# The sample outputs of three heads turned by VectorE blocks and GpSimd DMAs instead of TensorE transposes

## The chip, the cores and the metric

The kernel runs on one core of a Trainium2 chip. The metric is the device time of one execution in microseconds (us). Engines are named as the profile does: PE is TensorE (PEld its weight loads), DVE is VectorE, ACT is ScalarE, POOL is GpSimd, SP is SyncE, which here only issues DMAs.

## The reference, cut to what matters

One inference step of a two-layer decoder on a group of 256 prompt tokens and a group of 64 sample tokens (8 sequences of 8). Layer 0 mixes tokens by gated linear attention with four heads (key width 256, value width 512), layer 1 by a gMLP; each is followed by an MLP. The change lies in layer 0, in what follows the attention of the sample tokens:

```python
o = (jnp.einsum('bhtk,bhkv->bhtv', q_dec, s)
     + jnp.einsum('bhts,bhsv->bhtv', scores, vi))
...
o = o * lax.rsqrt(jnp.mean(jnp.square(o), axis=-1, keepdims=True) + HEAD_NORM_EPS) * norm_g
o = o.reshape(bsz, t, GLA_VAL_DIM).astype(x.dtype) * jax.nn.silu(r)
return o @ w_out, s_fin.astype(s0.dtype)
```

So for each head and token the 512 output values are squared and averaged, and the values are scaled by the inverse root of that mean before they go into the output projection.

## The kernel before, in words

Activations lie transposed in SBUF: features on the 128 partitions, the 320 tokens (256 prompt, 64 sample) along the free axis. Every projection is a run of **weight units**: `unit` loads 512 KB of float32 weights by a DMA of SyncE (`raw`, three buffers), ScalarE rounds them to `wh` (L144), VectorE makes the remainder `wl` (L145), each in a ring of four buffers, and TensorE does 24 matmuls with a unit (`mm3`, L161 to L163: low weights by high data, high by low, high by high). `group` runs over the units of one or two blocks of 256 columns and evicts the sums at the end.

The attention of a head is cut into **steps** (`Head.steps`), which are laid between the weight units. `Side` holds the list and is called after each unit; it takes `ceil(steps left / calls left)` steps from the front. The steps of head h run beside the projections `project_r` of head h and `project_v` of head h+1, 16 calls in all; those of the last head beside its `project_r` and the first two units of the output projection, 10 calls. The order of steps of a head: scores of sample and prompt tokens, then 16 sample steps (8 sequences by 2 key halves) with four prompt steps among them, then `sample_o`, `weigh`, `finish`.

A sample step (`sample_step`) adds into the PSUM tile `hd.po` the query times the carried state (L631, twice), makes the new state (L634 on TensorE, L635 on VectorE) and, for the second key half, stores it from the GpSimd queue (L638). `po` then holds tokens on the partitions and 512 values along the free axis: 64 rows of one partial sum and 64 rows of a second one, for the rounded part and the remainder. `sample_o` brings this into the layout of the rest: ScalarE copies `po` to `os_` (L643); TensorE transposes four 128x128 blocks (L646); ScalarE copies one partial sum to `o_all` (L649); VectorE adds the other (L650); ScalarE squares (L652); VectorE sums the four value blocks into `s1` (L653); a matmul with ones sums over the partitions (L656); `rsqrt` follows. `weigh` (L537) and `finish` (L543) scale `o_all`.

`gather` (L421) is an existing helper: after VectorE has transposed each 32x32 block in place of a full transpose, 16 DMAs (four calls with q = 0 to 3, four DMAs each) carry the blocks to the right partitions. It serves `va` (values, 32 KB a DMA) and `kz`, `ktp` (keys, 16 KB a DMA), on the GpSimd queue, in the last head partly on SyncE's.

Tiles of one tag share its buffers, one buffer in pool `gp`. So `os_` and the squares of the prompt lie in the buffer `sq`, and `kip` (prompt keys of a head, written by L427) has one buffer. The framework adds the waits. It also sets the **order in each engine's queue**: it is asked to plan with simulated times (`schedule_with_timeline_sim=True`, L1126), takes what it believes ready, and prefers what comes first in the program. On the chip each queue runs in that fixed order.

Of the kernel before, what the change touches and what calls it, by code (L numbers as in the profile page):

```python
# [8 lines left out]
F32 = mybir.dt.float32  # L9
# [6 lines left out]
P = 128  # L16
# [6 lines left out]
H = 4  # L23
DK, DV = 256, 512
# [53 lines left out]
def step_kernel(ctx: ExitStack, tc: tile.TileContext, A):  # L78
    nc = tc.nc
    uid = [0]  # L80

    def nm(s):
        uid[0] += 1
        return f"{s}_{uid[0]}"
# [22 lines left out]
    def gltile(n=512):  # L107
        return gl.tile([P, n], F32, tag="gl", name=nm("gl"), padded_shape=[P, 512])
# [4 lines left out]
    ident = cp.tile([P, P], F32, tag="ident", name="ident")  # L113
# [68 lines left out]
    def rsqrt(out, src, scale, eps, eps_t, pool):  # L182

        w = pool.tile([P, T], F32, tag="nw", name=nm("nw"), bufs=1)
        y = pool.tile([P, T], F32, tag="ny", name=nm("ny"), bufs=1)
        nc.scalar.activation(y[:], src, AF.Abs_reciprocal_sqrt, bias=eps_t[:], scale=scale)
        nc.vector.tensor_scalar(w[:], src, -0.5 * scale, -0.5 * eps, op0=ALU.mult, op1=ALU.add)
        nc.vector.tensor_mul(w[:], w[:], y[:])
        nc.vector.tensor_mul(w[:], w[:], y[:])
        nc.vector.scalar_tensor_tensor(out, w[:], 1.5, y[:], op0=ALU.add, op1=ALU.mult)  # L190
# [23 lines left out]
    gp = gst.enter_context(tc.tile_pool(name="gp", bufs=1))  # L214
# [120 lines left out]
    class Head:  # L335
# [284 lines left out]
        def sample_step(hd, b, kt):  # L620
# [16 lines left out]
            if kt == 1:  # L637
                nc.gpsimd.dma_start(SO[b, hd.h].rearrange("(k p) v -> p k v", p=P), st[:])  # L638

        def sample_o(hd):  # L640
            h, s1 = hd.h, hd.s1
            os_ = gp.tile([P, DV], F32, tag="sq", name=nm("os"))
            nc.scalar.copy(os_[:], hd.po[:])  # L643
            pt = gltile()
            for vt in range(4):
                nc.tensor.transpose(pt[:, vt * P : (vt + 1) * P], os_[:, vt * P : (vt + 1) * P], ident[:])  # L646
            pv = pt[:].rearrange("p (v c t) -> p v c t", v=4, c=2)
            o_s = o_all[:, 4 * h : 4 * h + 4, TP:T]
            nc.scalar.copy(o_s, pv[:, :, 0, :])  # L649
            nc.vector.tensor_add(o_s, o_s, pv[:, :, 1, :])  # L650
            sq = g2.tile([P, 4, DB * DS], F32, tag="vfm", name=nm("sq"), bufs=1)
            nc.scalar.activation(sq[:], o_s, AF.Square)  # L652
            nc.vector.tensor_reduce(s1[:, TP:T], sq[:].rearrange("p v t -> p t v"), axis=AX.X, op=ALU.add)  # L653

            pr = gltile(T)
            nc.tensor.matmul(pr[:], ones[:], s1[:], start=True, stop=True)  # L656
            hd.rs = gp.tile([P, T], F32, tag="rs", name=nm("rs"))
            rsqrt(hd.rs[:], pr[:], 1.0 / DV, HEAD_EPS, eps_h, gp)

        def steps(hd):  # L660

            yield hd.sample_scores
            yield hd.prompt_scores
            yield hd.sample_first
            sample = [lambda b=b, kt=kt: hd.sample_step(b, kt) for b in range(DB) for kt in range(2)]
            prompt = {0: lambda: hd.prompt_o(0), 2: lambda: hd.prompt_o(1),
                      12: lambda: hd.prompt_state(0), 14: lambda: hd.prompt_state(1)}
            for i, x in enumerate(sample):
                if i in prompt:
                    yield prompt[i]  # L670
                yield (lambda x=x, q=i - 4: (hd.gather_k(q), x())) if 0 <= i - 4 < 4 else x
            yield hd.sample_o
            yield hd.weigh
            yield hd.finish
# [330 lines left out]
    for j in range(KT):  # L1005
        if j % 4 == 0:
            steps.append(lambda j=j: mix4(j))
        steps.append(lambda j=j: mixed(j, *mix(j)))
    side = Side(steps, 6 * NU)
    ph, pl = yh, yl  # L1010

# [45 lines left out]
    for j in range(KT):  # L1057
# [5 lines left out]
        else:  # L1063
            if j not in ps:
                put_d(j)
            t = l2.tile([P, T], F32, tag="t", name=nm("t"), bufs=3)
# [70 lines left out]
```

## Time and profile before

| | |
|---|---|
| median of 3 runs | 2693.67 us (2693.67 to 2694.58) |
| the profiled execution | 2693.64 us |
| its span, first to last instruction | 2691.9 us |
| mean granted TensorE clock | 0.999 |
| TensorE busy | 2683.6 us |
| VectorE / ScalarE / GpSimd busy | 1547.4 / 1164.8 / 187.9 us |
| mean DMA rate | 164 GB/s |

The four heads lie in the first 450 us or so of the span; the `os_` copies of L643 start between 133.9 and 441.3 us. A row of a timeline gives start, length, engine, line, operation, what it writes and reads, how often, and in brackets how long its engine stood idle before it and what ended that. A row of a line's own view gives shortest, median and longest duration in ns. A row of waits names the waiting engine, tile and line, whom it waited for, the total in us, how often and the longest. A row of a stretch gives its bounds and length, then busy time and number of instructions of TensorE, its weight loads, VectorE, ScalarE and GpSimd, then the clock, the DMA share and GB/s. The row of a kind of DMA gives the size of one and the median time from issue to landing.

### The profile page before, as it was taken

The page shows a single profiled execution, that of the slowest core. Times are in us where ns is not written, and L with a number is a line of the kernel's source. Part 1 is how long each engine was busy: PE and PEld are TensorE (multiplying, and loading weights), DVE is VectorE, ACT ScalarE, POOL GpSimd, SP SyncE. Part 2 cuts the span into 40 slices and gives each one's busy share as a digit, 9 for nine tenths or more (in the row PEclk, how much of TensorE's full clock was granted, in tenths as well). Part 3 has the DMA queues.
Part 4 walks back from the last instruction along what each step waited for, and adds up shares of the span by engine and source line. Part 5 has one row for each costly group of instructions (what it writes and reads, how often), then busy time and mean ns, then how long its engine had stood idle before and what let it go on. Part 6 is the DMA issues. An engine that isn't in the chain of part 4 may idle for free.

```text
span 2691.9 us, 44835 instructions
## 1 busy us (share of the span) xinstructions
PE 2683.6 (100%) x18419; PEld 2661.3 (99%) x18419; DVE 1547.4 (57%) x2305; ACT 1164.8 (43%) x1646; POOL 187.9 (7%) x323
## 2 busy tenths in 40 slices
PE   9999999999999999999999999999999999999999
PEld 9999999999999999999999999999999999999998
DVE  7677677885445444444478765686444444444446
ACT  5455455564234334323446554355324333333434
POOL 4353341000000000000001000000000000000000
PEclk9999999999999999999999999999999999999999
DMA  8667667545444444445545544455445444444442
GB/s 252 220 196 249 218 193 258 187 141 163 151 151 154 150 154 152 153 153 151 155 148 158 160 139 139 136 164 151 155 149 155 151 152 154 150 156 149 153 153 79
DMA packets 136381, 440.84 MB, mean 164 GB/s; under 512 B 19824, under 2 KB 25840, under 8 KB 136176
## 3 DMA queue, kind: packets, MB, share of 16 engines
q1 hardware_dynamic: 121440, 408.08, 48.8%
q0 software_dynamic: 14192, 29.25, 3.5%
q8 instruction: 144, 2.36, 0.4%
q10 hardware_dynamic: 544, 0.66, 0.1%
q14 instruction: 61, 0.50, 0.1%
HBM read 409.60 MB, written 22.02 MB: 160 GB/s over the span
## 4 chain that ended last, share of the span: by engine, by line
PE 99%; DMA 0%; ACT 0%; DVE 0%; ACTq 0%; issue 0%; DVEq 0%
PE mm L161 32%; PE mm L163 32%; PE mm L162 31%; PE gl L631 1%; PE gl L634 1%; PE gl L589 1%; PE gl L980 0%; PE gl L573 0%; DMA raw<-gla_w_in 0%; ACT z L1070 0%; PE gl L975 0%; DMA xr<-xT 0%; PE gl L558 0%; PE gl L603 0%; PE gl L574 0%; PE gl L552 0%
## 5 line engine op out<-in xcount | busy, mean ns | idle before, releaser
L145 DVE TENSOR_TENSOR wl<-raw,wh 128x1024 fp32r<-128x1024 f32 (+1 forms) x740 | 901.0, 1219 | 944.4 <-ACT wh L144 942.5
L144 ACT CAST wh<-raw 128x1024 fp32r<-128x1024 f32 (+1 forms) x740 | 771.2, 1044 | 1231.5 <-PE mm L163 1121.3
L163 PE MATMUL mm<-yh,wh 128*128 128x320 f32 x2624 | 805.0, 307 | 0.0
L161 PE MATMUL mm<-yh,wl 128*128 128x320 f32 x2624 | 803.1, 308 | 0.0
L162 PE MATMUL mm<-yl,wh 128*128 128x320 f32 x2624 | 794.2, 303 | 0.0
L161 PE MATMUL mm<-hh,wl 128*128 128x320 f32 x2048 | 630.8, 308 | 0.0
L163 PE MATMUL mm<-hh,wh 128*128 128x320 f32 x2048 | 628.7, 307 | 0.0
L162 PE MATMUL mm<-hl,wh 128*128 128x320 f32 x2048 | 619.6, 303 | 0.0
L162 PEld LDWEIGHTS mm<-yl,wh 128*128 128x128 f32 x2624 | 492.6, 188 | 0.0
L161 PEld LDWEIGHTS mm<-yh,wl 128*128 128x128 f32 x2624 | 491.0, 188 | 0.0
L163 PEld LDWEIGHTS mm<-yh,wh 128*128 128x128 f32 x2624 | 490.8, 187 | 0.0
L162 PEld LDWEIGHTS mm<-hl,wh 128*128 128x128 f32 x2048 | 384.5, 188 | 0.0
L161 PEld LDWEIGHTS mm<-hh,wl 128*128 128x128 f32 x2048 | 384.4, 188 | 0.0
L163 PEld LDWEIGHTS mm<-hh,wh 128*128 128x128 f32 x2048 | 383.0, 187 | 0.0
L161 PE MATMUL mm<-xh,wl 128*128 128x320 f32 x768 | 237.9, 311 | 0.6 <-ACT xh L230 0.4
L163 PE MATMUL mm<-xh,wh 128*128 128x320 f32 x768 | 236.3, 309 | 0.0
L162 PE MATMUL mm<-xl,wh 128*128 128x320 f32 x768 | 235.2, 306 | 0.0
L162 PEld LDWEIGHTS mm<-xl,wh 128*128 128x128 f32 x768 | 144.2, 188 | 4.6 <-issue 1.2
L161 PEld LDWEIGHTS mm<-xh,wl 128*128 128x128 f32 x768 | 144.0, 188 | 4.7 <-issue 0.7
L163 PEld LDWEIGHTS mm<-xh,wh 128*128 128x128 f32 x768 | 143.6, 187 | 2.6 <-issue 0.7
L421 POOL DMA_DIRECT2D va<-blk x128 | 73.9, 585 | 79.9 <-DVE blk L482 52.0
L889 DVE TENSOR_TENSOR hl<-f,hh 128x320 fp32r<-128x320 f32 x128 | 61.9, 487 | 29.4 <-ACT hh L888 29.4
(261 smaller groups left out, 2209.7 us busy)
## 6 DMA issues: line engine op xcount, KB each, us to landing
raw<-mlp_w SPq DMA_DIRECT2D x512, 512.0 KB, 3.5
raw<-gla_w_in SPq DMA_DIRECT2D x94, 512.0 KB, 4.2
raw<-sg_w_in SPq DMA_DIRECT2D x64, 512.0 KB, 3.6
st<-state SPq DMA_DIRECT2D x32, 512.0 KB, 5.4
o_state_s<-st POOLq DMA_DIRECT2D x32, 512.0 KB, 4.1
raw<-gla_w_out SPq DMA_DIRECT2D x32, 512.0 KB, 4.4
raw<-sg_w_out SPq DMA_DIRECT2D x32, 512.0 KB, 3.5
va<-blk POOLq DMA_DIRECT2D x128, 32.0 KB, 4.3
```

What stands on the lines that cost most here:

```text
L144: nc.scalar.copy(hi[:, ks, :], raw[:, ks, :])
L145: nc.vector.tensor_sub(lo[:, ks, :], raw[:, ks, :], hi[:, ks, :].bitcast(F32))
L161: nc.tensor.matmul(ps, wl[:, kk, s], x_h, start=first, stop=False)
L162: nc.tensor.matmul(ps, wh[:, kk, s], x_l, start=False, stop=False)
L163: nc.tensor.matmul(ps, wh[:, kk, s], x_h, start=False, stop=last)
L421: queue.dma_start(out[32 * q : 32 * (q + 1), :, i, :], src[32 * i : 32 * (i + 1), :, q, :])
L589: nc.tensor.matmul(pairs(pu), hd.ktp[:, kt, blk, :], hd.v_prompt(blk), start=(blk == 0), stop=(blk == 1))
L631: nc.tensor.matmul(po[:], qm[:, kt, b * P : (b + 1) * P], part[:], start=False, stop=(b == DB - 1 and kt == 1 and part is sth))
L634: nc.tensor.matmul(pairs(pu), kz[:, i, kt, g, :], hd.v_sample(g), start=True, stop=True)
L889: nc.vector.tensor_sub(hl[:, j, 0:T], f[:], hh[:, j, 0:T].bitcast(F32))
```

## The change

`sample_o` is split. A new step `sample_out` copies `po` to `os_`; for the first three heads VectorE transposes its 32x32 blocks into `ob` (in the buffer of `kip`), and 16 GpSimd DMAs gather them into `ot` (in the buffer `sq`). Three steps that do nothing follow. `sample_o` then adds the two partial sums from `ot` in one VectorE instruction, and goes on as before. The last head keeps TensorE's transposes, made in `sample_out`, and has no empty steps.

```diff
+        def sample_out(hd):
+
+            os_ = gp.tile([P, DV], F32, tag="sq", name=nm("os"))
+            nc.scalar.copy(os_[:], hd.po[:])
+            if hd.h < H - 1:
+                ob = gp.tile([P, DV], F32, tag="kip", name=nm("ob"))
+                nc.vector.transpose(ob[:], os_[:])
+                hd.ot = gp.tile([P, DV], F32, tag="sq", name=nm("ot"))
+                for q in range(4):
+                    hd.gather(hd.ot[:], ob[:], q)
+            else:
+                hd.ot = gltile()
+                for vt in range(4):
+                    nc.tensor.transpose(hd.ot[:, vt * P : (vt + 1) * P], os_[:, vt * P : (vt + 1) * P], ident[:])
+
         def sample_o(hd):
             h, s1 = hd.h, hd.s1
-            os_ = gp.tile([P, DV], F32, tag="sq", name=nm("os"))
-            nc.scalar.copy(os_[:], hd.po[:])
-            pt = gltile()
-            for vt in range(4):
-                nc.tensor.transpose(pt[:, vt * P : (vt + 1) * P], os_[:, vt * P : (vt + 1) * P], ident[:])
-            pv = pt[:].rearrange("p (v c t) -> p v c t", v=4, c=2)
+            pv = hd.ot[:].rearrange("p (v c t) -> p v c t", v=4, c=2)
             o_s = o_all[:, 4 * h : 4 * h + 4, TP:T]
-            nc.scalar.copy(o_s, pv[:, :, 0, :])
-            nc.vector.tensor_add(o_s, o_s, pv[:, :, 1, :])
+            if h < H - 1:
+                nc.vector.tensor_add(o_s, pv[:, :, 0, :], pv[:, :, 1, :])
+            else:
+                nc.scalar.copy(o_s, pv[:, :, 0, :])
+                nc.vector.tensor_add(o_s, o_s, pv[:, :, 1, :])
...
+            yield hd.sample_out
+            if hd.h < H - 1:
+                for _ in range(3):
+                    yield lambda: None
             yield hd.sample_o
             yield hd.weigh
             yield hd.finish
```

## The prediction

> **What bounds the kernel now.** I read the page's first part, then who waited for whom on TensorE.
>
> ```profile
> span 2691.9 us, 44835 instructions
> PE 2683.6 (100%) x18419; PEld 2661.3 (99%) x18419; DVE 1547.4 (57%) x2305; ACT 1164.8 (43%) x1646; POOL 187.9 (7%) x323
> PE 99%; DMA 0%; ACT 0%; DVE 0%; ACTq 0%; issue 0%; DVEq 0%
> PE gl L152 <- DVE ones L116: 1.1, 1, 1.1
> PE mm L161 <- ACT xh L230: 0.4, 1, 0.4
> PE mm L161 <- DVE wl L145: 0.2, 1, 0.2
> ```
>
> TensorE is busy from end to end, the chain that ended last runs 99% through it, and in the whole span it waited for others for 1.7 us, all of it at the start-up lines or once for a weight. So the time is the number of TensorE's instructions times their spacing. An edit can gain what it takes off that queue; it can lose as much as it makes that queue wait, without limit. The work that hides everything else is the stream of weight units.
>
> **What leaves TensorE.** Twelve of the sixteen transposes of L646 go (four for each of three heads). Their rows, then the second head's four with their neighbours on TensorE, and the later sum over partitions (L656):
>
> ```profile
> L646 PEld LDWEIGHTS gl<-ident,os x16: 141/142/143, 137.2 to 444.8; 128*128 128x128 f32 x16
> L646 PE MATMUL gl<-ident,os x16: 272/273/273, 137.3 to 444.9; 128*128 128x128 f32 x16
> 242.59 0.30 PE L162 MATMUL mm<-xl,wh 128*128 128x320 f32 x1
> 242.74 0.31 PE L163 MATMUL mm<-xh,wh 128*128 128x320 f32 x1
> 242.88 0.60 PE L646 MATMUL gl<-ident,os 128*128 128x128 f32 x4
> 243.24 0.39 PE L161 MATMUL mm<-xh,wl 128*128 128x320 f32 x1
> 243.47 0.31 PE L162 MATMUL mm<-xl,wh 128*128 128x320 f32 x1
> 249.25 0.70 PE L656 MATMUL gl<-s,ones 128*128 128x320 f32 x2
> ```
>
> Matmuls start 0.145 us apart (242.59, 242.74), so without the transposes the L161 would start at 242.88 and the L162 at 243.03. It starts at 243.47. Four transposes therefore cost 0.44 us of the queue, not the 4 x 0.273 = 1.09 us that their lengths add up to, since they overlap one another and their neighbours. Three heads: **-1.3 us**. This is the one term with a sign that I am sure of.
>
> The Trainium skill, "TensorE: Matmul & The Clock Gate", Part 4 on PE-mode transpose, gives about 275 ns for a transpose inside a kernel. The record's 273 ns agrees with it as a length; taken as a price, it would make the gain 12 x 0.275 = 3.3 us. The spacing of the starts decides here, and I take 1.3.
>
> **What is added, and the chain it makes.** Per head: one VectorE block transpose of 128x512 (`ob`), 16 GpSimd DMAs of 16 KB, and a VectorE add that now waits for those DMAs. ScalarE's copy of `o_s` goes. The nearest rows: VectorE's transposes of half the width, the gathers of the same size and layout (`kz`, `ktp`), the rows of ScalarE and VectorE around the second head's sums, and the busy times of that stretch.
>
> ```profile
> 234.30 0.45 DVE L473 STREAM_TRANSPOSE blk<-mm 128x256 f32<-128x256 f32 x1
> L421 POOL DMA_DIRECT2D va<-blk x128: 582/582/640, 39.7 to 372.4; - x128
> L421 POOL DMA_DIRECT2D ktp<-blk x48: 548/549/569, 78.5 to 300.4; - x48
> ktp<-blk POOLq DMA_DIRECT2D x48, 16.0 KB, 3.3
> 239.43 0.58 ACT L643 COPY os<-gl 128x512 f32<-128x512 f32 x1
> 242.65 1.05 ACT L144 CAST wh<-raw 128x1024 fp32r<-128x1024 f32 x1 [2.64 <-PE mm L163]
> 243.60 0.36 ACT L649 COPY o_all<-gl 128x256 f32<-128x256 f32 x1
> 243.73 1.23 DVE L145 TENSOR_TENSOR wl<-raw,wh 128x1024 fp32r<-128x1024 f32 x1 [2.67 <-ACT wh L144]
> 244.87 0.41 DVE L650 TENSOR_TENSOR o_all<-o_all,gl 128x256 f32<-128x256 f32 x1
> 245.77 0.62 DVE L653 TENSOR_REDUCE s<-sq 128x64 f32<-128x256 f32 x1 [0.48 <-ACT sq L652]
> 274.35 0.41 DVE L427 TENSOR_TENSOR kip<-mm,ei 128x256 f32<-128x256 f32 x1
> 226.00:262.00 36.00, 36.00 (x235) 34.40 (x235) 27.47 (x49) 21.19 (x32) 15.97 (x27) 1.00 0.74 234
> ```
>
> *Engine time.* VectorE: 2 x 0.45 = 0.9 us per head, 2.7 us in all, beside 27.47 busy of 36. ScalarE: -0.36 us per head. GpSimd: 16 x 0.549 = 8.8 us per head, 26 in all, beside 15.97 of 36. DMA: 0.26 MB per head beside 234 GB/s x 36 us = 8.4 MB, 3% more. None of these engines is the bound, so I put all at nothing; the cover is the stream of weight units on TensorE, and without it they would cost their own lengths.
>
> *Where the steps fall.* A step is called after each weight unit: 24 matmuls, 24 x 0.145 = 3.5 us. For the first three heads 26 steps over 16 calls become 30. By the rule in `Side`, the last sample step sat after the 13th call and now sits after the 12th, with `sample_out` behind it; the empty steps fill the 13th call and half of the 14th; `sample_o` is after the 14th call, as before. So the chain starts 3.5 us earlier and gets two units, 7 us, between `os` and the sums. For the last head 26 steps become 27 over 10 calls: the last sample step moves one call up, and `sample_out` and `sample_o` fall into one call, with the same instructions as before. I price that at nothing, -0.5 to +0.5 us, as TensorE's total there is unchanged.
>
> *The chain in the second head, by the clock of the profile.* `os` ended at 240.0; 3.5 us earlier is 236.5. `ob` 0.9 us with a little for the hand-over: 237.5. Sixteen issues of 0.549 us: 246.3. The last lands 3.3 us later: **249.6**. From the add's start to the reduction's end took 244.87 to 246.39, 1.5 us, so the sums would be ready at **251.1** if the DMAs come first in GpSimd's queue. The sum's matmul stood at 249.25 in TensorE's queue. If the planner left it there, TensorE would wait 1.9 us; with the copy and the transposes gone the planner could even bring it about 1.5 us forward, to 247.8, and the wait would be 3.3 us.
>
> *What stands in front on GpSimd.* The next head's first sixteen `va` gathers wait for the same last sample step, and the last state store stands among them:
>
> ```profile
> 239.43 7.53 POOL L421 DMA_DIRECT2D va<-blk  x13 [7.97 <-PE gl L634]
> 247.49 0.72 POOL L638 DMA_DIRECT2D o_state_s<-st  x1 [0.53 <-issue]
> 248.21 1.75 POOL L421 DMA_DIRECT2D va<-blk  x3
> 257.44 4.60 POOL L421 DMA_DIRECT2D va<-blk  x8 [7.49 <-DVE blk L482]
> ```
>
> From 239.43 to 249.96 is 10.5 us, less 0.5 idle: 10.0. If all of it is queued ahead of the new sixteen, everything above is up to 9.5 us later: landed at about 259, sums at 260.6. If the new ones go first, `va` is 8.8 us later: done at about 256, when the next batch is not before 257.44, so nobody waits. `ob` lies in the slot of `kip`, which is next written at 274.35, beyond both cases.
>
> *Who waits behind the add.* VectorE's add holds up its `wl` splits, and ScalarE's square holds up its `wh` casts. The cast at 242.65 was let go by TensorE's finishing a unit, and fills a buffer four units on: TensorE reads it after three more units, about 242.65 + 3 x 3.5 + 1.0 = 254.1, while `wl` ended at 244.96. So VectorE can stand for some 9 us there before the weights are late (an estimate from these rows). The sum's matmul has no such reserve: TensorE's queue is in order.
>
> *Does the planner know?* It placed each engine's instructions by its own times, and the add and the sum's matmul move back if it expects the DMAs to land late. What it thinks a gather takes shows in the first head, where it slipped `ktp` gathers between state stores:
>
> ```profile
> 87.75 0.74 POOL L638 DMA_DIRECT2D o_state_s<-st  x1 [4.97 <-DVE st L635]
> 88.50 2.73 POOL L421 DMA_DIRECT2D ktp<-blk  x5
> 94.97 0.72 POOL L638 DMA_DIRECT2D o_state_s<-st  x1 [3.75 <-DVE st L635]
> 95.69 1.66 POOL L421 DMA_DIRECT2D ktp<-blk  x3
> 99.39 0.72 POOL L638 DMA_DIRECT2D o_state_s<-st  x1 [2.04 <-DVE st L635]
> ```
>
> Four more `ktp` gathers were still to come at 91, yet it put only five between stores 7.2 us apart and three between stores 4.4 us apart, and on the chip GpSimd stood idle 3.75 and 2.04 us after them. So it reckons about 1.2 us a gather, twice the chip's 0.55. Then it expects the sixteen to take some 19 us, and puts add and sum later than the chip needs them. Against it: thirteen `va` gathers stand ahead of the store at 247.49, whose data were there at about 239.9; at 1.2 us each that fits badly, and at 0.1 us well. The five-and-three pattern gives the price more directly, so I take **0 us** for the wait, and keep 3.3 to 12.8 us per head as the other end (251.1 and 260.6 less 247.8).
>
> A second rule speaks against the change. The gathers of the trace ran beside a VectorE busy 76% of the stretch above, and the slowest of the 128 `va` took 640 ns where the median took 582. The Trainium skill, "SBUF — State Buffer", section "SBUF: two separate sides", says that certain VectorE copies lock GpSimd out while it writes descriptors, with 620 ns growing to 3100 ns. By it, as an estimate, the sixteen could take 16 x 3.1 = 50 us; no issue in these rows does that.
>
> **The sum.** -1.3 (transposes) + 0 (engines, DMAs, last head) + 0 (wait) = -1.3 us. The profiled execution took 2693.64 us (span 2691.9 and 1.7 around it), the median of the runs is 2693.67, the same to 0.03. Forecast **2692.3 us**, 0.05% under. A change of 0.2% is 5.4 us: about what a measurement of this kernel can tell from none.
>
> **The rivals.**
> *A late gather stops TensorE.* The planner keeps the sum's matmul near 248 on this clock, and the chip's DMAs land after 246.3. Three heads at 3.3 to 12.8 us: +10 to +38, less 1.3: **2702 to 2731 us**, likeliest at the low half, about 2710. It decides from the point at which the sum's matmul is planned earlier than 13.6 us after `ob` is written. For it: the thirteen `va`. Against it: the price of 1.2 us.
> *The gain isn't kept.* TensorE's 0.44 us per head come back as short waits on the re-planned queue (a table load, a step in another place): **2693.6**.
> *The transposes are worth their length.* 12 x 0.273 = 3.3 us: **2690.4**. Against it: the spacing of the starts.
> *GpSimd slowed by VectorE.* The longest gap inside a run of gathers in the first head is quoted here, on top of the issue's own 0.58:
>
> ```profile
> 136.07 6.33 POOL L421 DMA_DIRECT2D va<-blk  x11 [1.47 <-issue]
> ```
>
> If every one of the sixteen met that, each would take 2.05 us, 33 us together: landed at 273.8, sums at 275.3, against 249.25 a wait of 26 us per head: **2770 us**. It happened once, so the chance is small. The SBUF page of the Trainium skill, cited above, leads to the same place.
>
> **How the numbers follow.** Forecast 0.70 (own range 2691.0 to 2693.5), gain not kept 0.08, transposes at full length 0.05, late gather 0.13, GpSimd slowed 0.02, and 0.02 for a gain above 5.4 us, for which I see no work to remove. Slower by over 0.2% takes the late gather and the slowed GpSimd: 0.15. Within 0.2% (2688.3 to 2699.1): 0.70 + 0.08 + 0.05 = 0.83. Faster: 0.02. The range takes the first three cases and a late gather that is mostly hidden: 2690.4 to 2700.0.
>
> **What would show it.** Twelve L646 records fewer and four left. In the second head: `os` near 236, `ob` one 128x512 transpose of about 0.9 us, sixteen gathers of 0.55 us, landing 12 us after the first issue; the add and the sum's matmul later than 249.25, at 251 or beyond, with no idle of TensorE before it. Wrong if TensorE waits at the sum's matmul or for a `wl` around 245 to 262 and its like in the other heads, or if GpSimd's issues stretch beyond 0.64 us.

## The result, and the profile after

The changed kernel takes **2737.51 us** (2736.65 to 2738.09, 4 runs) against 2693.73: a ratio of 1.0161, 95% interval 1.0149 to 1.0173. It is 43.8 us slower; the forecast was 2692.3. Its profiled execution took 2737.76 us.

From the page and from TensorE's waits over the whole span (engine and line, whom it waited for; us in total, times, longest):

```profile
span 2736.0 us, 44875 instructions
PE 2687.4 (98%) x18407; PEld 2665.5 (97%) x18407; DVE 1552.7 (57%) x2308; ACT 1166.0 (43%) x1643; POOL 214.2 (8%) x371
PE mm L161 <- DVE qd L459: 39.6, 3, 13.2
PE gl L152 <- DVE ones L116: 1.1, 1, 1.1
PE mm L161 <- ACT xh L230: 1.0, 1, 1.0
```

The twelve transposes are gone (18407 matmul records for 18419). In their place TensorE stands still three times, 13.2 us each, and not where the prediction looked: it waits for VectorE's `qd` (L459), the eviction of the *next* head's query projection, whose PSUM banks the next weight matmuls need. The chain that leads there, in the first of the three places, from the timelines of VectorE, ScalarE and TensorE:

```profile
166.00 1.23 DVE L145 TENSOR_TENSOR wl<-raw,wh 128x1024 fp32r<-128x1024 f32 x1 [2.24 <-ACT wh L144]
167.14 0.42 DVE L660 TENSOR_TENSOR o_all<-ot 128x256 f32<-128x256 f32 x1
171.66 0.70 PE L669 MATMUL gl<-s,ones 128*128 128x320 f32 x2
171.95 0.70 PE L369 MATMUL gl<-glow,wg 96*128 96x320 f32 x2
172.96 1.28 ACT L186 ACT_TABLE_LOAD   x1
174.68 0.94 ACT L370 ACTIVATE eb<-gl,vec 128x320 f32<-128x320 f32 x2
182.62 1.02 DVE L386 TENSOR_TENSOR ee<-eb 128x256 f32<-128x256 f32 x4
183.56 1.69 DVE L543 TENSOR_TENSOR o_all<-o_all,rs 128x320 f32<-128x320 f32 x4
185.31 0.49 DVE L459 SCALAR_TENSOR_TENSOR qd<-mm,eb 128x320 f32<-128x320 f32 x1
185.85 0.63 PE L161 MATMUL mm<-xh,wl 128*128 128x320 f32 x1 [13.20 <-DVE qd L459]
186.28 0.47 PE L162 MATMUL mm<-xl,wh 128*128 128x320 f32 x1
186.55 0.47 PE L163 MATMUL mm<-xh,wh 128*128 128x320 f32 x1
```

The add (L660) comes at 167, the sum's matmul (now L669) at 171.7, and right behind it the next head's gate matmul (L369). From that matmul on there are 13 us of work on ScalarE and VectorE before `qd` is written: the previous head's inverse root (from 172.96) and its `finish` (L543), and the gate's own exponentials, logarithms and scans. Before, the same two matmuls stood here:

```profile
143.69 0.70 PE L656 MATMUL gl<-s,ones 128*128 128x320 f32 x2
148.29 0.45 PE L369 MATMUL gl<-glow,wg 96*128 96x320 f32 x2
```

So the sum moved back by 28 us, and the gate, which has nothing to do with the sample outputs, by 24. In the order of TensorE's queue, both now come after all 192 weight matmuls of the key and query projection: 960 weight matmuls lie ahead of them from the start of the program, where it was 764 and 792. Nothing that can run without the gate is left.

Nor did TensorE or the add wait for a gather on the chip. GpSimd and VectorE around the second head:

```profile
254.56 0.71 DVE L646 STREAM_TRANSPOSE ob<-os 128x512 f32<-128x512 f32 x1 [1.33 <-ACT os L643]
253.83 8.08 POOL L421 DMA_DIRECT2D va<-blk  x14 [1.40 <-PE gl L631]
261.96 1.10 POOL L421 DMA_DIRECT2D ot<-ob  x2
272.52 1.09 POOL L421 DMA_DIRECT2D ot<-ob  x2 [0.16 <-issue]
ot<-ob POOLq DMA_DIRECT2D x48, 16.0 KB, 5.6
287.79 0.42 DVE L660 TENSOR_TENSOR o_all<-ot 128x256 f32<-128x256 f32 x1
```

The last gather was issued by 273.6 and, by its landing in the trace, had landed at 277.4. The add stands at 287.79 with no wait in its row. In the first and third head the last gather landed at 159.1 and 399.0, and the add starts at 167.14 and 407.99. So the add's place in VectorE's queue was planned later than the chip needed, by 8 to 10 us.

The last part of the loss is in the rows at 186: matmuls 0.267 us apart instead of 0.145. The clock by stretches (the last three columns are the granted clock, the DMA share and GB/s):

```profile
172.00:186.00 14.00, 0.80 (x5) 0.46 (x3) 9.47 (x23) 11.75 (x19) 0.00 (x0) 0.60 0.35 114
186.00:192.00 6.00, 6.00 (x23) 6.00 (x24) 5.93 (x27) 0.92 (x4) 0.53 (x1) 0.52 0.00 0
192.00:206.00 14.00, 14.00 (x112) 13.37 (x111) 7.01 (x14) 5.77 (x10) 13.00 (x25) 1.00 0.42 106
```

After the three stops 22, 17 and 14 matmuls run at half the clock. At 0.122 us each that is about 6.5 us. 39.6 + 6.5 - 1.3 = 44.8, against a span 44.1 us longer; the remaining 0.7 us I did not trace.

### The profile page after: what moved, and what is told of

Its sections match the earlier page's. It is cut to its first block, busy times and chain, and to the rows that moved or that the text cites. A ratio compares the mean times of both kernels' runs of the same rounds, so it can differ in the third digit from the quotient of the medians.

```text
span 2736.0 us, 44875 instructions
## 1 busy us (share of the span) xinstructions
PE 2687.4 (98%) x18407; PEld 2665.5 (97%) x18407; DVE 1552.7 (57%) x2308; ACT 1166.0 (43%) x1643; POOL 214.2 (8%) x371
## 4 chain that ended last, share of the span: by engine, by line
PE 97%; ACT 1%; DVE 1%; DMA 0%; issue 0%; ACTq 0%; DVEq 0%
PE mm L161 32%; PE mm L163 31%; PE mm L162 31%; PE gl L631 1%; PE gl L634 1%; PE gl L589 1%; PE gl L997 0%; PE gl L573 0%; DMA raw<-gla_w_in 0%; ACT z L1087 0%; PE gl L992 0%; DMA xr<-xT 0%; DVE eb L383 0%; ACT wh L144 0%; ACT L381 0%; ACT L373 0%
## 5 line engine op out<-in xcount | busy, mean ns | idle before, releaser
L161 PE MATMUL mm<-xh,wl 128*128 128x320 f32 x768 | 240.3, 314 | 40.8 <-DVE qd L459 39.6
```

The lines of the kernel that those rows point to most:

```text
L161: nc.tensor.matmul(ps, wl[:, kk, s], x_h, start=first, stop=False)
```

## The experiments

**Theory.** The planner expects the gathers to land late and so puts the add, the square, the reduction and the sum's matmul far back. The gate matmul of the next head takes a PSUM buffer of the same four (`gl`), allotted in program order, so it can't pass the sum. Late gate, late evictions, full PSUM banks, idle TensorE, and then half clock. **Rivals:** the gathers or their traffic; the split step and the empty steps; VectorE and ScalarE held up by the add.

*Without the gathers.*

```diff
-                hd.ot = gp.tile([P, DV], F32, tag="sq", name=nm("ot"))
-                for q in range(4):
-                    hd.gather(hd.ot[:], ob[:], q)
+                hd.ot = ob
```

> The changed kernel without its sixteen DMAs per head: the add reads ob itself, so the three heads' sample values are in the wrong places. Theory (the planner prices the gathers high, puts add, square, reduction and the sum's matmul behind them, and the next head's gate matmul, whose PSUM buffer is allotted behind that of the sum, goes late with it): without DMAs nothing is late, no idle of TensorE, 12 transposes saved at 0.11 us: 2692.4 us, -1.3 against before. Rival (the splitting of the step and the empty steps cost the time): stays near 2737. Rival (transposes worth their length): 2690.4.

2693.23 us, before 2693.84 (ratio 0.9997, 0.9988 to 1.0006). The 44 us are gone, with the split and the empty steps still there. Only half of the 1.3 us came; TensorE's waits show what took the rest:

```profile
PE mm L161 <- DVE nw L187: 0.8, 1, 0.8
```

That is the last head's inverse root, a wait that the kernel before doesn't have.

*The same, the last head with 26 steps again* (`sample_out` called from its `sample_o`).

> The kernel without the gathers (add reads ob, values in the wrong places), and the last head's copy and transposes back inside its sample_o, so that the last head has 26 steps again. Theory (the 0.8 us wait of TensorE on the inverse root of the last head, seen without gathers, comes from the shifted steps): the wait vanishes, 2692.5 us, 1.3 under before, which is what 12 transposes are worth. Rival (the transposes are worth only 0.6): 2693.2. Rival (worth their length): 2690.4.

2692.78 against 2694.12: -1.34 us (ratio 0.9996, 0.9987 to 1.0005, so the difference of the medians is within what the interval allows). The wait is gone, and the medians of 11 and 21 runs differ by the 1.3 us that the starts of the matmuls gave; but the interval also holds 0, 0.6 and 3.3. The traces say it more sharply. The gate matmul has the same matmuls ahead of it before and without the gathers, but for the transposes. Its rows in the first and fourth head, first of the kernel before, then of the run without gathers:

```profile
40.89 0.46 PE L369 MATMUL gl<-glow,wg 96*128 96x320 f32 x2
359.42 0.46 PE L369 MATMUL gl<-glow,wg 96*128 96x320 f32 x2
40.94 0.46 PE L369 MATMUL gl<-glow,wg 96*128 96x320 f32 x2
358.28 0.46 PE L369 MATMUL gl<-glow,wg 96*128 96x320 f32 x2
```

From the first gate to the fourth, 318.53 us become 317.34: twelve transposes are worth 1.19 us, 0.1 each, and not 3.3.

*The sum in a PSUM buffer of its own.*

```diff
-    gl = gls.enter_context(tc.tile_pool(name="gl", bufs=4, space=bass.MemoryType.PSUM))
+    gl = gls.enter_context(tc.tile_pool(name="gl", bufs=3, space=bass.MemoryType.PSUM))
+    gr = gls.enter_context(tc.tile_pool(name="gr", bufs=1, space=bass.MemoryType.PSUM))
...
-            pr = gltile(T)
+            pr = gr.tile([P, T], F32, tag="gr", name=nm("pr"), padded_shape=[P, 512])
```

> The changed kernel, the sum's matmul in a PSUM buffer of its own (three shared buffers and this one, in place of four shared). Theory: the gate matmul no longer stands behind the sum; it goes 168 weight matmuls earlier in the first head, and the three 13 us stops before the q eviction vanish, so the time falls by at least 30 us, to about 2694 to 2705 (three shared buffers may cost something of their own). Rival (the gates are late because VectorE and ScalarE are held by the late add): the stops stay, 2737.

2735.14 (ratio 1.0152, 1.0138 to 1.0166): missed by 30 us in time, and close to the rival's time. The trace, lines one higher than before, says which half of the expectation held:

```profile
147.33 0.46 PE L370 MATMUL gl<-glow,wg 96*128 96x320 f32 x2
173.52 0.70 PE L670 MATMUL pr<-s,ones 128*128 128x320 f32 x2
298.67 1.03 PE L604 MATMUL gl<-qd,kis 128*128 128x32 f32 x4 [3.49 <-DVE kis L429]
493.98 0.63 PE L162 MATMUL mm<-oh,wl 128*128 128x320 f32 x1 [4.96 <-DVE wl L146]
PE mm L162 <- DVE qd L460: 7.5, 2, 5.0
PE gl L604 <- DVE kis L429: 6.9, 2, 3.5
```

After the first head the gate goes 26 us ahead of the sum, which stays at 173.5, and TensorE has no stop there at all: the PSUM order is what tied them, and the rival's stop isn't there. But the sum is still late, and the lateness now comes out elsewhere. TensorE's new waits add up to some 26 us, mostly for `qd` and `kis` in the second and third head, and for a weight and the sums in the last. The second head's steps run 18 us later in the clock than before; its own late add is followed at once by the next `kip` and `kis` (the add at 297.44, `kip` at 297.78), and `ob` lies in the buffer of `kip`; that the buffer is the link was not tried. The last head's steps then run into the output projection, with stops of 2.0 and 4.96 us. Curing one coupling moved the cost to the others.

*The next head's gates in place of the empty steps.*

```diff
-                for _ in range(3):
-                    yield lambda: None
+                yield from hds[hd.h + 1].gates()
...
-            hd.project_kq(Side(gates, 2 * NU))
+            hd.project_kq(Side([], 2 * NU))
```

> The changed kernel with the next head's three gate steps in place of the three empty steps, so that they stand ahead of the sum in the program. Theory: the gates are done before the sum is planned, no stop at the q eviction; but the next head's score matmuls now come behind the late sum for PSUM, so its steps run late: 2693 to 2705. Rival (VectorE and ScalarE held): 2737.

2702.76 (ratio 1.0033, 1.0021 to 1.0045). Four fifths of the loss vanish, with the same gathers on the same queue. What is left is mostly the last head, whose steps are late for the output projection:

```profile
457.32 0.91 PE L669 MATMUL gl<-s,ones 128*128 128x320 f32 x2 [2.09 <-DVE s L666]
462.99 0.64 PE L161 MATMUL mm<-oh,wl 128*128 128x320 f32 x1 [4.76 <-DVE wl L145]
```

*The kernel before, with its gates late.* The gate steps are taken out of `project_kq`'s list and called as its k eviction begins. No gather, no split step.

```diff
                 if n == 0:
                     side.flush()
+                    for g in late:
+                        g()
...
-            hd.project_kq(Side(gates, 2 * NU))
+            hd.project_kq(Side([], 2 * NU), gates)
```

> The kernel before, TensorE's transposes and all, with one edit: the next head's three gate steps are called only when the k eviction begins, so that the gate matmul comes behind the last weight matmul that can run without an eviction, where the changed kernel has it. No gathers, no late sum. Theory (the late gate alone makes the loss): three stops of some 11 us (13.2 less the 1.8 us of root and table load in front of the gates), each followed by about 24 matmuls at half clock (2.7 us): 2694 + 3 x 14 = 2736 us, 2728 to 2742. Rival (the late gate is only a sign, the gathers or their traffic make the loss): within 5 us of 2694.

2727.77 (ratio 1.0125, 1.0111 to 1.0138): 33.8 us slower, just below the range.

```profile
PE mm L161 <- DVE qd L459: 29.0, 3, 9.7
182.72 0.64 PE L161 MATMUL mm<-xh,wl 128*128 128x320 f32 x1 [9.68 <-DVE qd L459]
```

The same wait at the same three places, 9.7 us where I had worked out 11. A late gate alone makes 34 of the 44 us. The 3.5 us by which each stop is shorter are mostly the previous head's inverse root and its `finish`, 1.7 us on VectorE right ahead of `qd`, which stand inside the chain of the changed kernel (172.96 and 183.56 above) and not here.

*Four gathers instead of sixteen.*

```diff
-                for q in range(4):
+                nc.vector.memset(hd.ot[:], 0.0)
+                for q in range(1):
                     hd.gather(hd.ot[:], ob[:], q)
```

> The changed kernel with four of the sixteen gathers (q = 0), the rest of ot set to zero by VectorE, so most sample values of the three heads are left out. In TensorE's queue the gate matmul then comes 56, 80 and 56 weight matmuls earlier than in the changed kernel, 8.1, 11.6 and 8.1 us. Theory: each stop of 13.2 us is shorter by that: 5.1, 1.6 and 5.1 us, half clock after the longer ones: 2694 - 1 + 12 + 3 to 8 = 2708 to 2713. Rival (a fixed cost of having gathers there at all): 2730 or more.

2709.93 (ratio 1.0060, 1.0045 to 1.0075).

```profile
178.25 0.63 PE L161 MATMUL mm<-xh,wl 128*128 128x320 f32 x1 [5.64 <-DVE qd L459]
287.70 0.42 PE L161 MATMUL mm<-xh,wl 128*128 128x320 f32 x1 [2.18 <-DVE qd L459]
287.96 0.31 PE L162 MATMUL mm<-xl,wh 128*128 128x320 f32 x1
288.10 0.31 PE L163 MATMUL mm<-xh,wh 128*128 128x320 f32 x1
398.51 0.64 PE L161 MATMUL mm<-xh,wl 128*128 128x320 f32 x1 [5.65 <-DVE qd L459]
```

Stops of 5.64, 2.18 and 5.65 us for 5.1, 1.6 and 5.1 expected: the length of each stop follows from the gate's place in TensorE's queue. This is the strongest single result. It also bears on the planner: in the first head 739 weight matmuls lie ahead of the sum without gathers, 904 with four and 960 with sixteen, so most of the lateness comes with the first four, and it isn't proportional to the number of gathers.

*Without the empty steps* (one execution).

> The changed kernel without the three empty steps. The order in every engine's queue is the same as in the changed kernel, so theory: the same time, about 2737 us. Rival (the empty steps put the sums late): under 2720.

2737.59, and the trace has the same three waits for `qd`, 39.6 us in all. The empty steps neither cause nor cure anything.

*The gathers on other queues.* SyncE (`nc.sync` as the queue of `gather`), then SyncE with the gates ahead and the last head's 26 steps, then the same with ScalarE, ScalarE without moving the gates, and half on each:

> The changed kernel with the sixteen gathers issued by SyncE. In the order of TensorE's queue the sum and the gate matmul then come 142 weight matmuls (20 us) earlier than in the changed kernel. Theory: no stop at the q eviction. SyncE's queue carries the weight loads, and sixteen issues of 0.6 us are 9.6 us in it per head, against about three units of 3.5 us loaded ahead: 2692.5 if that hides them, up to 2710 if it doesn't. Rival (gathers land late on the chip, whichever queue): 2720 or more.

> The same with the gathers on SyncE. Theory: what SyncE's gathers cost by delaying weight loads stays as in the run with SyncE alone, about 3 to 5 us; 2695 to 2699. If the gates were what still waited there: 2692.4.

> Next head's gates in place of the empty steps, last head with 26 steps, the gathers issued by ScalarE. In TensorE's queue the sum comes 133 weight matmuls (19 us) earlier than in the changed kernel and the next scores stand where they stood before. Theory: no stop behind the sum; ScalarE gives 16 x 0.6 = 9.6 us per head to issuing, against about 9 us of reserve: 2692.4 if it hides, up to 2706 if the casts come late. Rival (SBUF and PSUM couplings beyond the sum and the gates): 2715 or more.

> The changed kernel with the gathers issued by ScalarE, gates where they were, last head with 26 steps. The sum and the gate matmul come together 132 weight matmuls earlier than in the changed kernel, 132 before the last one that can run without an eviction. Theory: no stop at the q eviction; as the run with the gates ahead, 2692.4 to 2706. Rival (the gate behind the sum stops TensorE wherever it stands): 2715 or more.

> Next head's gates in place of the empty steps, last head with 26 steps, eight gathers per head from SyncE and eight from ScalarE, 4.8 us on each queue. Theory: half of what each alone cost is inside its reserve: 2692.5 to 2696, at best 1.3 under before. Rival (what costs is the gathers' landing, whichever queue): as with SyncE alone, 2697 or more.

| gathers on | gates | us | ratio, 95% interval |
|---|---|---|---|
| SyncE | in place | 2699.39 | 1.0019, 1.0010 to 1.0028 |
| SyncE, last head 26 steps | ahead | 2697.05 | 1.0011, 1.0002 to 1.0020 |
| ScalarE, last head 26 steps | ahead | 2706.24 | 1.0042, 1.0029 to 1.0054 |
| ScalarE, last head 26 steps | in place | 2707.02 | 1.0046, 1.0033 to 1.0060 |
| both, last head 26 steps | ahead | 2697.10 | 1.0011, 1.0002 to 1.0020 |

On these queues the plan puts the sum 132 to 144 weight matmuls earlier in the first head, and the 13 us stops are gone even where the gate still stands directly behind the sum. The two ScalarE runs and the half on each came 0.2 to 1.1 us above their ranges, the half on each inside that of its rival. What remains is another thing on each queue, by TensorE's waits: ScalarE with gates in place (two lines), SyncE with gates ahead, both.

```profile
PE mm L161 <- DVE wl L145: 4.9, 3, 2.8
PE mm L161 <- DVE kis L428: 3.4, 3, 1.7
PE mm L161 <- DVE vst L478: 3.1, 2, 1.6
PE mm L161 <- DVE wl L145: 2.2, 1, 2.2
```

ScalarE with gates in place, in the first head:

```profile
134.82 12.65 ACTq L421 DMA_DIRECT2D ot<-ob  x16
150.29 0.45 PE L161 MATMUL mm<-xh,wl 128*128 128x320 f32 x1 [2.85 <-DVE wl L145]
```

Sixteen issues hold ScalarE for 12.65 us, 0.8 each for the 0.6 that I took, and the weights come late: there the price of issuing is seen. With half on each, too, TensorE's one new wait above 0.2 us is for a weight and none is for a gather, which speaks against the rival. With SyncE and the gates ahead it waits for the eviction of the values (`vst`); what delays that was not followed. None of the versions with gathers beats the kernel before.

## Why the prediction was wrong

- *Transposes, -1.3 us.* Right: by the places of the gate matmul twelve are worth 1.19 us, and the row of starts gave 1.32. The length rival would need 3.3.
- *Engines and DMAs at nothing.* TensorE waited for none of the added work in the changed kernel. The gathers were under-sized: 14 us from the first issue to the last in the first head (141.8 to 155.5), not 8.8, since GpSimd also waited for earlier DMAs to land; and 5.6 us to landing, not 3.3. In this plan it didn't matter, since the add stood 8 to 10 us behind the last landing. It would matter in a better one: with those 8 to 10 us taken off, sum and gate would stand 55 to 72 weight matmuls earlier, which is about where the run with four gathers has them, and that run is still 16 us slower than before. So by this estimate, which no run tests, the true latency alone costs about a third of the loss as long as the gate stays behind the sum.
- *Where the steps fall, and GpSimd's order.* The 3.5 us of head start didn't come: in the first head `os` starts at 133.57, before at 133.87, and in TensorE's queue the last sample step moved by 1 to 6 weight matmuls, not 24. In the second head all sixteen `va` but two went first, the bad case of the two that I had. From `ob` to the last landing the three heads took 22 to 24 us, where that case gave 21.5.
- *The last head at nothing.* Right for the changed kernel, whose TensorE has no new wait there. In the run without gathers it was 0.8 us of waiting, just beyond the 0.5 allowed.
- *"Does the planner know?"* This is the step that failed, in its conclusion. I read from the stores between the `ktp` gathers that the planner reckons a gather at about twice its time, and that the add and the sum would therefore be put "later than the chip needs them". That is what happened: the sum came 28 us later than before. (The price itself isn't shown: two thirds to three quarters of the shift, by head, come with the first four of the sixteen gathers.) But I then took 0 us for it, as though a late place in the queue cost nothing. I asked who would wait behind the add on VectorE and ScalarE, and never who stands behind the sum on TensorE: the next head's gate matmul, behind the same PSUM buffers, with 13 us of serial work hanging on it. What I took as 0 us measured 39.6 us of waiting and some 6.5 us lost at half clock. The signs of being wrong that I named looked in the wrong place, too: in the three heads TensorE waited neither at the sum's matmul nor for a `wl`.
- *The late-gather rival* had the right sign and the right three heads, with a wrong place and mechanism: TensorE had no stop at the sum's matmul, and the add waited for no gather's landing. Its upper end, 2731, was still under the result, because the next head's late gate wasn't in it.
- *GpSimd slowed by VectorE.* The `ot` issues took 549 ns in the median and 561 at most, so neither the rival nor the rule of the Trainium skill's "SBUF — State Buffer", section "SBUF: two separate sides", came into play here.

## What to carry to other kernels

When a planner orders the queues, its belief in a long latency is itself a cost: the consumer is put late, and whatever shares its buffers in program order goes late with it, even work that has no data in common. Ask for each moved step who takes the next buffer of the same pool, and how long a chain hangs on that. A saving of 1.3 us isn't worth a latency of more than 20 us on a path that another head's work is queued behind.

## What the runs showed of the hardware

A stop of TensorE costs more than its length. After the 13.2 us stops, matmuls started 0.267 us apart for 4 to 6 us, after the first at a granted clock of 0.52; after 5.64 us the same; after 2.18 us none did (the rows at 287.70 above). The Trainium skill, "TensorE: Matmul & The Clock Gate", section "Why this matters for your kernels", advises no idle gaps of more than about 3 us between matmul bursts, or the clock falls to half; these stops lie on the sides that it says. Two shorter stops don't: in the run with the sum's own buffer one of 2.53 us, which ends at 279.46, and in the run with the gathers on SyncE, gates in place, one of 1.92 us, which ends at 276.07. Each was followed, a little later, by a stretch at a lower clock:

```profile
282.00:285.00 3.00, 3.00 (x15) 3.00 (x15) 0.28 (x2) 0.00 (x0) 2.32 (x4) 0.63 1.03 301
278.00:281.00 3.00, 3.00 (x14) 3.00 (x14) 3.00 (x9) 1.35 (x2) 0.00 (x0) 0.57 0.92 283
```

So the bound isn't sharp at 3 us here. In the traces' records of the granted clock, the stretches at half clock behind these stops last 3.41 us or a whole multiple of it: 17.07, 13.65 and 13.65 us for the three stops of the changed kernel, beginning inside the stop, and 3.41 us behind each of the two short ones.
